# A two-block transformer kernel: one class of 21 places for weights and working tiles, in place of many classes and hand-written sequences

## The chip, the cores and the metric

The kernel runs on one core of a Trainium2 chip. The metric is the device time of one execution in microseconds (us). The profile of one execution shows the engines TensorE (PE, with its weight loads PEld), VectorE (DVE), ScalarE (ACT), GpSimd (POOL) and SyncE (SP), and the DMA queues.

## The reference

256 tokens of 1024 features, in fp32, pass two blocks. The first block has two layers, the second block one:

```python
def first_block(x, ...):
    h = x
    for l in range(DEPTH):          # DEPTH = 2
        h = h + hybrid_mixer(rmsnorm(h, norm_mix[l]), w_in[l], w_branch_a[l], w_branch_b[l],
                             b_gate[l], sink_logit[l], w_out[l])
        h = h + expert_choice_ffn(rmsnorm(h, norm_ffn[l]), w_router[l], w_expert_gate[l],
                                  w_expert_up[l], w_expert_down[l])
    return rmsnorm(h, norm_final)

def second_block(x, c, ctx, ...):
    x = x + sincos_2d(x.shape[1])
    ...
    x_mix, _, _ = token_mixer(modulate(rms_norm(x, norm1_g), sh1, sc1) @ w_in, ...)
    x = x + gt1 * x_mix
    x = x + gt2 * hier_moe(modulate(rms_norm(x, norm2_g), sh2, sc2), ...)
    return rms_norm(x, final_norm_g)
```

`hybrid_mixer` is a dilated attention and a windowed attention with a gate for each, projected by w_out. In `expert_choice_ffn` each of 16 experts takes its best 32 tokens (gate and up, 1024 x 2048, silu, down 1024 x 1024). `token_mixer` is a gated linear attention beside a long convolution; `hier_moe` has 32 experts of width 512 in 4 groups, of which each token uses 2 of one group. The weights are read once, some 750 MB in all.

## The kernel before

All weights come as chunks of 128 x 2048 fp32 (1 MB), by `Core.chunk`, whose DMA is issued by SP (`piece`, L60). A chunk can also come as four pieces of 128 x 512 in small tiles (`quarters`, L68). All other DMAs of the kernel are on SP too. The products of the mixers are made in three passes of split numbers (`mm3`, L118 to L120): ACT writes the high part `wh` (L98), DVE or POOL the low part `wl` (L99); the small classes wh and wl have three tiles of 128 x 512 each, P and PT four. The experts multiply without a split (L774, L816; in the second block L1429, L1470).

SBUF holds 19 places of 8 KB per partition for chunks and big working tiles. They are classes by tag: w (5), x (4) and ten single ones, hTa, hTb, qa, qb, qc, V, G, hgw, hn and ob. A working tile (queries, values, gates, the normed tokens) names its tag. A chunk takes its tag from `K.spare`, a list written for the stage, and when that is empty from `K.ring`, a sequence that goes round. Both are written out by hand for each stage:

```python
    own = ("hn", "ob") if ahead else ("G", "V")
    K.ring = list("wwxwx")
    K.spare = [None] * 7 + ["V", "qa", "qb", "qc"] + ([] if ahead else ["ob"]) + ["hgw"] + (["G"] if ahead else [])
    K.spare += [("P",) * 4] + ([] if ahead else ["hn"]) + [("wh", "wh", "wh", "wl"), ("wl", "wl", "PT", "PT")]
```

A tile framework finds the waits between the instructions and fixes the order of the instructions on each engine beforehand, from a plan of times of its own. A tile of a class gets a place when the place's last tenant is done with, and the tiles of one class get their places in the order in which the program writes them first. Classes are independent of each other in this.

The stages in order: `mixer` of layer 0 and `experts` of layer 0, with part of the next layer's mixer done within (`Ahead`); the same for layer 1, with preparations of the second block within (`prep`); `token_mixer`; `moe` with `moe_round` and `moe_quad`; `final`. At the end of a mixer comes w_o in two halves of 512 columns (c = 0, 1); `route` transposes the finished half of h (L190), copies it to `hTr` and multiplies it by the router (L659) between the two. Then `experts` has the scaled tokens `ht2` written (`scaled_tokens`, L677), makes the one-hot matrices, gathers each expert's tokens in `xT`, and runs over 16 experts of 8 chunks (w_eg) and 4 x 16 chunks of w_ed. `moe` writes its scaled tokens as `ht0` and `ht1` (L109) and then runs over 8 quads of 16 chunks w2eg and 8 of w2ed. Between routing and experts stand the chunks of the modulation (`ada`, and `gb` at L599).

Of the kernel before, what the change touches and what calls it, by code (L numbers as in the profile page):

```python
# [32 lines left out]
class Core:  # L33
    def __init__(self, ctx, tc, A):
        self.tc, self.nc, self.A = tc, tc.nc, A
        self.const = ctx.enter_context(tc.tile_pool(name="const", bufs=1))
        self.sb = ctx.enter_context(tc.tile_pool(name="sb", bufs=1))
        self.ps = ctx.enter_context(tc.tile_pool(name="ps", bufs=1, space=PSUM))
        self.flip = self.nsplit = self.nchunk = 0
        self.after = nullcontext  # L40
        self.ring, self.spare, self.idle = list("wwxwx"), [], ()
# [33 lines left out]
    def t(self, shape, name, bufs=1, tag=None, dt=F):  # L75
        return self.sb.tile(shape, dt, name=name, tag=tag or name, bufs=bufs)
# [134 lines left out]
class Ahead:  # L211
# [78 lines left out]
RING = {"w": 5, "x": 4}  # L290
# [25 lines left out]
def mixer(K, h, l, ada, first=None, ahead=None):  # L316
# [142 lines left out]
    if ahead:  # L459
        K.ring = list("wwwwwx")  # L460

    def window():
# [155 lines left out]
def first_loads(K):  # L618
# [3 lines left out]
    K.sink, K.bgate = K.load("sink", [128, L, 16, 2]), K.load("bgate", [128, L, 16])  # L622
# [3 lines left out]
    K.iota, K.fold = K.load("iota", [128, 65]), K.load("fold", [128, 96])  # L626
# [54 lines left out]
def experts(K, h, l, mix, ada, prep, ahead=None):  # L681
# [74 lines left out]
    K.ring = list("wwxwx")  # L756
    K.spare = [None] * 7 + ["V", "qa", "qb", "qc"] + ([] if ahead else ["ob"]) + ["hgw"] + (["G"] if ahead else [])
    K.spare += [("P",) * 4] + ([] if ahead else ["hn"]) + [("wh", "wh", "wh", "wl"), ("wl", "wl", "PT", "PT")]
    hid, Ge = [], []
    gw = K.t([128, 4], "gw4")  # L760
    for e in range(NE):
        if e == 2:
            for _ in gather(1):
                pass
            K.ring = ["w", "x", "w", "V", "w", "x", "qb", "w", "qc", "x", "w", "hgw", "x", "G"] if ahead else list("wwxwx") + ["qc"]
        oh, xT = ohs[e // 8], xTs[e // 8]
        gu = K.bank("mm")
        for k in range(KD):
# [3 lines left out]
            w = K.chunk(A["w_eg"][l, e, k])  # L772
# [34 lines left out]
    K.ring = ["w", "x", "w", "qc", "w", "x", "w", "x", "w"] if ahead else ["w", "x", "w", "qc", "w", "hTa", "x", "w", "qa", "w"]  # L807
# [25 lines left out]
    K.ring = list("wwxwx")  # L833
# [22 lines left out]
def context(K):  # L856
# [24 lines left out]
    s0 = K.t([128, PW], "S0", tag="x", bufs=RING["x"])  # L881
# [47 lines left out]
def long_filter(K):  # L929
# [29 lines left out]
    dec, hs = K.t([128, 4, 512], "dec", tag="hgw"), K.t([128, 4, 512], "hs", tag="x", bufs=RING["x"])  # L959
# [24 lines left out]
def token_mixer(K, h):  # L984
# [22 lines left out]
    cb = K.t([128, 4, 256], "cb", tag="cA")  # L1007
# [49 lines left out]
    xa = K.t([128, 8, T], "xa", tag="x", bufs=RING["x"])  # L1057
    xb = K.t([128, 8, T], "xb", tag="x", bufs=RING["x"])
# [12 lines left out]
    def hyena():  # L1071
# [29 lines left out]
        y = K.t([128, 2, 4, T], "yb", tag="x", bufs=RING["x"], dt=FR)  # L1101
# [176 lines left out]
def moe(K, h, mix):  # L1278
# [22 lines left out]
    lg = K.t([128, 2, 36], "lg2")  # L1301
# [3 lines left out]
    s = K.t([128, 2, 64], "rsm")  # L1305
# [16 lines left out]
    tmp = K.t([128, 2, NE2], "rtmp")  # L1322
# [4 lines left out]
    ix = K.t([128, 2, 8], "ix")  # L1327
# [86 lines left out]
def moe_quad(K, h, xT, oh, cmb, e, i, gate):  # L1414
# [45 lines left out]
    for hf in range(2):  # L1460
# [3 lines left out]
        wd = [K.chunk(A["w2ed"][e + x, hf]) for x in range(3 if end else 4)]  # L1464
# [94 lines left out]
def constants():  # L1559
# [15 lines left out]
    o["iota"] = np.broadcast_to(np.arange(65, dtype=f), (128, 65))  # L1575
# [30 lines left out]
def pack_first(i):  # L1606
# [28 lines left out]
    o["sink"] = np.broadcast_to(i["sink_logit"][None, :, :, None], (128, L, 16, 2))  # L1635
# [60 lines left out]
```

## Time and profile before

| | us |
|---|---|
| median of 3 runs (lowest, highest) | 2268.3 (2260.67, 2269.16) |
| the profiled execution | 2264.96 |
| its span | 2263.2 |
| PE busy | 1810.0 (80%) |
| PEld busy | 1026.7 (45%) |
| DVE busy | 786.9 (35%) |
| ACT busy | 588.7 (26%) |
| POOL busy | 220.7 (10%) |

The DMA queue of SP moved 745.82 MB; its packets took 81.7% of the 16 DMA engines' span. A DMA share near 1 in a stretch says that the 16 engines were busy throughout. A row of a timeline is one instruction, or several of a form in sequence (x7): start, time from the first to the end of the last, line, operation, output and input. A row of SP is the issue of a DMA, not its transfer. In brackets stands the idle time before an instruction and what ended it.

### The profile page before, as it was taken

The numbers are of one execution on the slowest core, as the hardware profiler recorded it, in microseconds if no ns is written. First come the engines' busy times: TensorE is split into PE (matmuls) and PEld (weight loads), VectorE is DVE, ScalarE is ACT, GpSimd is POOL, SyncE is SP. The second block draws the span as 40 slices with busy tenths as digits, with TensorE's granted clock in tenths as the row PEclk, the third lists the DMA queues.
The fourth block names the chain that finished last, engine by engine and source line by source line (L and its number), as shares of the span: only waits on it lengthen the run. The fifth ranks groups of instructions, "written<-read, shape, count | busy, mean of one in ns | idle before, by whom it ended". The sixth has DMA issues, their size and how long they took to land.

```text
span 2263.2 us, 30298 instructions
## 1 busy us (share of the span) xinstructions
PE 1810.0 (80%) x12172; PEld 1026.7 (45%) x12172; DVE 786.9 (35%) x1823; ACT 588.7 (26%) x1182; POOL 220.7 (10%) x179
## 2 busy tenths in 40 slices
PE   8999997666699998996778566669999877776765
PEld 8877741111277765842234223248888522121211
DVE  5766620000145589631211111147647511111112
ACT  5545510000033345620124200036325310000000
POOL 2111200000011122200000000024224100000000
PEclk9999997777799999998899777889999999999999
DMA  7446599999999944679999999982336799999996
GB/s 301 136 165 238 216 377 421 421 421 422 422 375 409 386 163 187 233 278 366 411 416 415 371 420 421 420 336 105 119 115 233 300 411 421 421 421 421 422 421 277
DMA packets 113626, 748.87 MB, mean 331 GB/s; under 512 B 14695, under 2 KB 15112, under 8 KB 25416
## 3 DMA queue, kind: packets, MB, share of 16 engines
q1 hardware_dynamic: 112936, 745.82, 81.7%
q8 instruction: 98, 1.61, 0.3%
q10 hardware_dynamic: 544, 1.05, 0.1%
q14 instruction: 48, 0.39, 0.1%
HBM read 745.77 MB, written 1.05 MB: 330 GB/s over the span
## 4 chain that ended last, share of the span: by engine, by line
PE 44%; DMA 27%; issue 21%; DVE 5%; ACT 2%; POOL 0%; POOLq 0%; SPq 0%; DVEq 0%; ACTq 0%
DMA w<-in_w_eg 15%; DMA w<-in_w_ed 7%; PE mm L118 7%; PE mm L120 7%; PE mm L119 6%; PE mm L774 4%; PE acc L816 4%; DMA w<-in_w2z 1%; DVE wl L99 1%; PE acc L493 1%; PE acc L901 1%; PE sc L841 1%; DMA w<-in_ada 1%; PE acc L1181 1%; PE sc L478 1%
## 5 line engine op out<-in xcount | busy, mean ns | idle before, releaser
L774 PE MATMUL mm<-w,xT 128*32 128x512 f32 x2048 | 325.0, 743 | 131.4 <-DMA w<-in_w_eg 131.3
L98 ACT ACTIVATE wh<-w 128x512 fp32r<-128x512 f32 x384 | 239.5, 630 | 314.5 <-PE mm L119 237.1
L118 PE MATMUL mm<-hTa,wh 128*128 128x256 f32 x960 | 282.5, 296 | 8.3 <-DVE qa L242 2.4
L120 PE MATMUL mm<-hTa,wl 128*128 128x256 f32 x960 | 276.4, 291 | 4.5 <-DVE wl L99 4.2
L119 PE MATMUL mm<-hTb,wh 128*128 128x256 f32 x960 | 274.4, 287 | 1.2 <-DVE hTb L1004 1.2
L99 DVE TENSOR_TENSOR wl<-w,wh 128x512 fp32r<-128x512 f32 x286 | 220.1, 775 | 100.4 <-ACT wh L98 97.5
L1429 PE MATMUL mm<-w,xT 128*32 128x512 f32 x1024 | 174.1, 618 | 61.5 <-DMA w<-in_w2eg 60.9
L99 POOL TENSOR_TENSOR wl<-w,wh 128x512 fp32r<-128x512 f32 x98 | 129.7, 1324 | 917.2 <-ACT wh L98 411.8
L774 PEld LDWEIGHTS mm<-w,xT 128*32 128x32 f32 x2048 | 59.1, 123 | 352.3 <-DMA w<-in_w_eg 245.3
L816 PE MATMUL acc<-w,hid 128*32 128x256 f32 x2048 | 167.0, 436 | 59.9 <-DMA w<-in_w_ed 59.9
L118 PEld LDWEIGHTS mm<-hTa,wh 128*128 128x128 f32 x960 | 182.8, 191 | 28.4 <-issue 13.5
L120 PEld LDWEIGHTS mm<-hTa,wl 128*128 128x128 f32 x960 | 182.5, 191 | 14.3 <-issue 6.2
L119 PEld LDWEIGHTS mm<-hTb,wh 128*128 128x128 f32 x960 | 183.5, 191 | 5.4 <-issue 2.4
L816 PEld LDWEIGHTS acc<-w,hid 128*32 128x32 f32 x2048 | 76.8, 124 | 136.2 <-DMA w<-in_w_ed 68.2
L1470 PE MATMUL acc<-w,work 128*32 128x512 f32 x512 | 103.4, 681 | 36.4 <-DMA w<-in_w2ed 35.0
L1429 PEld LDWEIGHTS mm<-w,xT 128*32 128x32 f32 x1024 | 33.6, 110 | 172.1 <-DMA w<-in_w2eg 126.1
L175 POOL TENSOR_TENSOR rs<-rs,mhalf 128x2 f32<-128x2 f32 x9 | 6.7, 748 | 1010.7 <-DVE rs L174 1010.5
L790 DVE TENSOR_TENSOR hid<-tp,sg 128x256 f32<-128x256 f32 x32 | 13.6, 424 | 221.0 <-ACT sg L789 221.0
L88 DVE COPY gs<-mm 128x512 f32<-128x512 f32 x16 | 11.1, 692 | 199.6 <-PE mm L774 199.6
L110 DVE SCALAR_TENSOR_TENSOR yd<-acc,gw,yd 128x256 fp32r<-128x256 f32 x32 | 15.5, 483 | 179.4 <-ACT yd L109 179.4
L789 ACT ACTIVATE sg<-tp 128x256 f32<-128x256 f32 x32 | 12.3, 383 | 227.5 <-PE tp L786 227.4
L109 ACT ACTIVATE yd<-acc,gw 128x256 fp32r<-128x256 f32 x32 | 15.1, 473 | 213.2 <-PE acc L816 213.2
(469 smaller groups left out, 2504.4 us busy)
## 6 DMA issues: line engine op xcount, KB each, us to landing
w<-in_w_eg SPq DMA_DIRECT2D x250, 1024.0 KB, 15.6
w<-in_w_ed SPq DMA_DIRECT2D x128, 1024.0 KB, 14.1
w<-in_w2eg SPq DMA_DIRECT2D x126, 1024.0 KB, 19.8
w<-in_w2ed SPq DMA_DIRECT2D x63, 1024.0 KB, 19.8
w<-in_ada SPq DMA_DIRECT2D x24, 1024.0 KB, 6.3
w<-in_w_in SPq DMA_DIRECT2D x22, 1024.0 KB, 7.1
w<-in_wk SPq DMA_DIRECT2D x20, 1024.0 KB, 9.3
w<-in_w_b SPq DMA_DIRECT2D x8, 1024.0 KB, 6.2
```

The costliest lines, as they stand in the source:

```text
L98: self.hi = nc.scalar.activation(hi, src, AF.Copy)
L99: (nc.gpsimd if n in self.idle or n % 4 == 3 else nc.vector).tensor_tensor(lo, src, hi.bitcast(F), OP.subtract)
L118: mm(out, lhsT=l[0], rhs=r[0], start=start, stop=False)
L119: mm(out, lhsT=l[0], rhs=r[1], start=False, stop=False)
L120: mm(out, lhsT=l[1], rhs=r[0], start=False, stop=stop)
L478: nc.tensor.matmul(p[:, sl], lhsT=q[hq], rhs=KL[hq, kv // 2, :], start=False, stop=True)
L493: nc.tensor.matmul(po[half * 64:half * 64 + 64, :T], lhsT=V[:, kt, c:c + 64], rhs=PTs[half][:, kt * 256:(kt + 1) * 256], start=(kt == 0), ...
L774: nc.tensor.matmul(gu[32 * j:32 * j + 32, :], lhsT=xT[:, k, (e % 8) * CAP:(e % 8 + 1) * CAP], rhs=w[:, j * 512:(j + 1) * 512], start=(k == ...
L816: nc.tensor.matmul(dn[32 * x:32 * x + 32, :T], lhsT=hid[e // 8][:, e % 8, f, hh * 32:hh * 32 + 32], rhs=ws[x][:, fb * T:(fb + 1) * T], sta ...
L841: nc.tensor.matmul(p[:, :T], lhsT=hn[:, tt, kb * 128:(kb + 1) * 128], rhs=oh[:, tt].rearrange("p a b -> p (a b)"), start=(tt == 0), stop=( ...
L1429: nc.tensor.matmul(gu[o:o + 32, :], lhsT=xT[:, k, y:y + CAP2], rhs=ws[x][:, (2 * kk + j) * 512:(2 * kk + j + 1) * 512], start=(k == 0), st ...
L1470: nc.tensor.matmul(dn[32 * x:32 * x + 32, :], lhsT=hid[x][:, c, :], rhs=wd[x][:, c * 512:(c + 1) * 512], start=(c == 0), stop=(c == 3), ti ...
```

## The change

All big working tiles and all whole chunks have one tag, "W", with 21 places; the hand-written sequences are gone. `experts` requests the first 21 chunks (19 whole, the ninth and tenth as quarter pieces) before the tiles that it gathers into, and `moe` does so with 16 chunks of w2eg and 3 of w2ed. The two further places come from a smaller reserve for dynamic DMAs (`dynamic_dma_scratch_size`, to 1024), a sink constant without its doubled column, a shorter iota, and small tiles of `moe` that lie in a free part of `cb`.

```diff
-        self.ring, self.spare, self.idle = list("wwxwx"), [], ()
+        self.idle, self.spare = (), []
...
-        tag = self.spare.pop(0) if self.spare else None
-        if tag is None:
-            tag = self.ring[self.nchunk % len(self.ring)]
-            self.nchunk += 1
-        if isinstance(tag, tuple):
-            return self.quarters(src, tag)
-        return self.piece(src, tag)
-
-    def piece(self, src, tag):
-        t = self.sb.tile([128, PW], F, name="w", tag=tag, bufs=RING.get(tag, 1))
+        if self.spare and (tags := self.spare.pop(0)):
+            return self.quarters(src, tags)
+        t = self.sb.tile([128, PW], F, name="w", tag="W", bufs=PLACES)
         self.nc.sync.dma_start(out=t[:, :src.shape[1]], in_=src)
         return t
+
+    def next_chunk(self, src):
+        return self.pre.pop(0) if self.pre else self.chunk(src)
...
     def t(self, shape, name, bufs=1, tag=None, dt=F):
-        return self.sb.tile(shape, dt, name=name, tag=tag or name, bufs=bufs)
+        tag = tag or name
+        if tag in WHOLE:
+            tag, bufs = "W", PLACES
+        return self.sb.tile(shape, dt, name=name, tag=tag, bufs=bufs)
...
-RING = {"w": 5, "x": 4}
+
+WHOLE = {"x", "hTa", "hTb", "qa", "qb", "qc", "V", "G", "hgw", "hn", "ob"}
+PLACES = 21
+SPARE = [None] * 8 + [("P", "P", "wh", "wh"), ("wh", "wl", "wl", "wl")]
...
-                sk = K.sink[:, l, hd, :]
+                sk = K.sink[:, l, hd:hd + 1].to_broadcast([128, 2])
...
     own = ("hn", "ob") if ahead else ("G", "V")
-    K.ring = list("wwxwx")
-    K.spare = [None] * 7 + ["V", "qa", "qb", "qc"] + ([] if ahead else ["ob"]) + ["hgw"] + (["G"] if ahead else [])
-    K.spare += [("P",) * 4] + ([] if ahead else ["hn"]) + [("wh", "wh", "wh", "wl"), ("wl", "wl", "PT", "PT")]
+    K.spare = SPARE[:]
+
+    ws = [K.chunk(A["w_eg"][l, i // KD, i % KD]) for i in range(PLACES)]
...
-            w = K.chunk(A["w_eg"][l, e, k])
+            w = ws.pop(0) if ws else K.chunk(A["w_eg"][l, e, k])
...
-    cb = K.t([128, 4, 256], "cb", tag="cA")
+    cb = K.t([128, 5, 256], "cb", tag="cA")
+    K.small = cb[:, 4]
...
-    K.spare = ["x"] * 3
     ada_gate(K, 0)
-    K.ring, K.spare = ["w"], [None] * 4 + ["x"] * 3
...
-    K.spare = ["qa", "V", "qb", "G", "hgw", "x", "x", "ob", "x", "w", ("wh", "wh", "wh", "wl"),
-               ("wl", "wl", "PT", "PT"), "qc", "w", "w", "w", "w"]
-    K.ring = ["qa", "w", "qb", "hgw", "w", "x", "ob", "w", "x", "qc", "w", "x", "w"]
+    K.spare = SPARE[:]
+    K.pre = [K.chunk(A["w2eg"][0 + 2 * i + x, c]) for i in range(2) for c in range(4) for x in range(2)]
+    K.pre += [K.chunk(A["w2ed"][x, 0]) for x in range(3)]
...
-            ws = [K.chunk(A["w2eg"][e + 2 * pr + x, c]) for x in range(2)]
+            ws = [K.next_chunk(A["w2eg"][e + 2 * pr + x, c]) for x in range(2)]
...
-    nc = bacc.Bacc("TRN2", target_bir_lowering=False, num_devices=1)
+    nc = bacc.Bacc("TRN2", target_bir_lowering=False, num_devices=1, dynamic_dma_scratch_size=1024)
```

Five more assignments of `K.ring` in the stages are removed in the same way, and tiles that named `RING["x"]` drop it.

## Rows read from the trace of the kernel before

**Rows 1.** The page: the span.

```profile
span 2263.2 us, 30298 instructions
```

**Rows 2.** Stretches: window, us; busy PE, PEld, DVE, ACT, POOL; PEclk, DMA share, GB/s.

```profile
230.00:300.00 70.00, 65.36 (x376) 45.15 (x374) 38.48 (x87) 27.96 (x54) 15.52 (x14) 0.93 0.59 224
300.00:640.00 340.00, 234.91 (x1518) 68.72 (x1516) 29.29 (x59) 25.35 (x51) 2.58 (x2) 0.78 1.01 419
640.00:800.00 160.00, 153.95 (x1432) 118.17 (x1430) 84.00 (x130) 50.98 (x89) 21.04 (x16) 0.98 0.95 384
...
1250.00:1270.00 20.00, 12.21 (x68) 5.42 (x68) 5.69 (x19) 9.58 (x12) 0.00 (x0) 0.66 0.71 279
```

**Rows 3.** The chain of waits: start us, length us, what was waited for.

```profile
366.83 19.82 DMA w<-in_w_eg
```

**Rows 4.** DMA issues, 60 to 300 us: the queue's total; count, size, us to landing.

```profile
q1 hardware_dynamic: 7950, 46.91, 53.4%
...
w<-in_w_eg SPq DMA_DIRECT2D x19, 1024.0 KB, 6.1
...
w<-in_w_eg SPq DMA_DIRECT2D x6, 256.0 KB, 6.8
```

**Rows 5.** DMA issues, 810 to 1034 us.

```profile
q1 hardware_dynamic: 9192, 47.12, 56.8%
...
w<-in_w_eg SPq DMA_DIRECT2D x26, 1024.0 KB, 6.6
...
w<-in_w_eg SPq DMA_DIRECT2D x12, 256.0 KB, 8.9
```

**Rows 6.** DMA issues, 1510 to 1820 us.

```profile
q1 hardware_dynamic: 9163, 55.19, 47.3%
...
w<-in_w2eg SPq DMA_DIRECT2D x19, 1024.0 KB, 6.7
```

**Rows 7.** SP's timeline, 230 to 300 us: start, us, what is issued.

```profile
230.73 35.59 SPq L60 DMA_DIRECT2D w<-in_w_eg  x7
266.90 3.37 SPq L68 DMA_DIRECT2D w<-in_w_eg  x6
```

**Rows 8.** ACT's timeline, 270 to 285 and 1774 to 1786 us: first writes of ht.

```profile
275.36 2.54 ACT L677 ACTIVATE ht<-h,rs 128x512 f32<-128x512 f32 x4
...
1781.62 2.56 ACT L109 ACTIVATE ht<-h,rs 128x512 fp32r<-128x512 f32 x4 [0.49 <-POOL rs L175]
```

**Rows 9.** SP's waits, 230 to 300 us: us in total, times, longest.

```profile
SPq L68 <- PE mm L120: 1.8, 3, 0.7
```

**Rows 10.** PE's timeline, 250 to 270 us: w_o (sc, mm) and route's transposes (tp).

```profile
254.13 0.64 PE L118 MATMUL sc<-wh,mTa 128*128 128x512 f32 x2
...
258.33 0.38 PE L190 MATMUL tp<-ident,h 128*128 128x128 f32 x2
...
260.59 0.64 PE L118 MATMUL mm<-wh,mTa 128*128 128x512 f32 x2
...
261.99 0.63 PE L118 MATMUL mm<-wh,mTa 128*128 128x512 f32 x2
...
269.27 0.40 PE L120 MATMUL mm<-wh,mTb 128*128 128x512 f32 x1
```

**Rows 11.** SP's timeline, 930 to 1034 us.

```profile
973.46 2.89 SPq L68 DMA_DIRECT2D w<-in_w_eg  x5
979.17 20.86 SPq L60 DMA_DIRECT2D w<-in_w_eg  x6
```

**Rows 12.** PE's and SP's timelines, 1740 to 1822 us.

```profile
1775.86 0.64 PE L118 MATMUL mm<-wh,mTa 128*128 128x512 f32 x2
...
1778.17 1.40 SPq L68 DMA_DIRECT2D w<-in_w2eg  x3
1786.66 2.04 SPq L60 DMA_DIRECT2D w<-in_w2eg  x3
```

**Rows 13.** DVE's timeline, 1465 to 1530 us: the wait is in brackets.

```profile
1496.16 2.36 DVE L994 TENSOR_TENSOR hg<-h,gf 128x1024 f32<-128x1024 f32 x2 [8.03 <-DMA gf<-in_gfin]
```

More of the change, by code (lines that the diff above doesn't have):

```diff
@@ L223, in start @@
         self.Ga, self.Gb = K.t([128, 8, T], "Ga", tag="G"), K.t([128, 8, T], "Gb", tag="hgw")
-        self.raw = K.t([128, 8, T], "raw", RING["x"], tag="x")
+        self.raw = K.t([128, 8, T], "raw", tag="x")
     def dest(self, j):
@@ L458, in mixer @@
     ob = (K.t([128, 8, T], "ob0", tag="hn", dt=FR), K.t([128, 8, T], "ob1", tag="ob", dt=FR))
-    if ahead:
-        K.ring = list("wwwwwx")
     def window():
@@ L517, in gates @@
             yield
-    QS = [K.t([128, 8, T], "q0", tag="qc", dt=FR), K.t([128, 8, T], "q1", RING["x"], tag="x", dt=FR)]
-    kx = K.t([128, 8, T], "kx", RING["x"], tag="x", dt=FR)
+    QS = [K.t([128, 8, T], "q0", tag="qc", dt=FR), K.t([128, 8, T], "q1", tag="x", dt=FR)]
+    kx = K.t([128, 8, T], "kx", tag="x", dt=FR)
     KK, KL = kx[:, 0:4, :].rearrange("p (x j) t -> p x j t", x=2), kx[:, 4:6, :]
@@ L606, in spread_gate @@
     if g == 0:
-        K.gt = K.t([128, PW], "gt", tag="x", bufs=RING["x"]).rearrange("p (a b) -> p a b", a=2)
+        K.gt = K.t([128, PW], "gt", tag="x").rearrange("p (a b) -> p a b", a=2)
     for c in range(2):
@@ L621, in first_loads @@
     nc.sync.dma_start(out=K.negd, in_=A["negd"])
-    K.sink, K.bgate = K.load("sink", [128, L, 16, 2]), K.load("bgate", [128, L, 16])
+    K.sink, K.bgate = K.load("sink", [128, L, 16]), K.load("bgate", [128, L, 16])
     K.gffn = K.load("gffn", [128, L, KD])
@@ L625, in first_loads @@
     nc.sync.dma_start(out=K.wr, in_=A["wr"])
-    K.iota, K.fold = K.load("iota", [128, 65]), K.load("fold", [128, 96])
+    K.iota, K.fold = K.load("iota", [128, CAP2 + 1]), K.load("fold", [128, 96])
     ada_setup(K)
@@ L764, in experts @@
                 pass
-            K.ring = ["w", "x", "w", "V", "w", "x", "qb", "w", "qc", "x", "w", "hgw", "x", "G"] if ahead else list("wwxwx") + ["qc"]
         oh, xT = ohs[e // 8], xTs[e // 8]
@@ L806, in experts @@
             K.copy(Ge[-1].rearrange("p a b -> p (a b)"), p)
-    K.ring = ["w", "x", "w", "qc", "w", "x", "w", "x", "w"] if ahead else ["w", "x", "w", "qc", "w", "hTa", "x", "w", "qa", "w"]
     for q in range(4):
@@ L832, in experts @@
                 next(prep, None)
-    K.ring = list("wwxwx")
 def gather_x(K, xT, hn, oh, gain, bias=None):
@@ L880, in context @@
     yield
-    s0 = K.t([128, PW], "S0", tag="x", bufs=RING["x"])
+    s0 = K.t([128, PW], "S0", tag="x")
     K.S0 = s0[:, :1024].rearrange("p (d h v) -> p d h v", d=2, h=HG)
@@ L958, in long_filter @@
     nc.sync.dma_start(out=w3, in_=A["hw3"])
-    dec, hs = K.t([128, 4, 512], "dec", tag="hgw"), K.t([128, 4, 512], "hs", tag="x", bufs=RING["x"])
+    dec, hs = K.t([128, 4, 512], "dec", tag="hgw"), K.t([128, 4, 512], "hs", tag="x")
     nc.sync.dma_start(out=dec, in_=A["decay"])
@@ L1056, in token_mixer @@
     weave((project_qv(), 16), (scans(), 8))
-    xa = K.t([128, 8, T], "xa", tag="x", bufs=RING["x"])
-    xb = K.t([128, 8, T], "xb", tag="x", bufs=RING["x"])
+    xa = K.t([128, 8, T], "xa", tag="x")
+    xb = K.t([128, 8, T], "xb", tag="x")
     hy = [xa[:, 0:4, :], xa[:, 4:8, :], xb[:, 0:4, :]]
@@ L1100, in hyena @@
                 yield
-        y = K.t([128, 2, 4, T], "yb", tag="x", bufs=RING["x"], dt=FR)
+        y = K.t([128, 2, 4, T], "yb", tag="x", dt=FR)
         for c in range(4):
@@ L1300, in moe @@
     cmb, msk, slot = R[:, 0], R[:, 1], R[:, 2]
-    lg = K.t([128, 2, 36], "lg2")
+    lg = K.small[:, 0:72].rearrange("p (t e) -> p t e", t=2)
     for tt in range(2):
@@ L1304, in moe @@
                                        op0=OP.mult, op1=OP.add)
-    s = K.t([128, 2, 64], "rsm")
+    s = K.small[:, 72:168].rearrange("p (t e) -> p t e", t=2)
     m, sm, pg, den = s[:, :, 0], s[:, :, 1], s[:, :, 2], s[:, :, 3]
@@ L1321, in moe @@
     le = lg[:, :, NG:36].rearrange("p t (g e) -> p t g e", g=NG)
-    tmp = K.t([128, 2, NE2], "rtmp")
+    tmp = K.small[:, 168:232].rearrange("p (t e) -> p t e", t=2)
     nc.vector.tensor_tensor(tmp.rearrange("p t (g e) -> p t g e", g=NG), le,
@@ L1325, in moe @@
     nc.vector.tensor_reduce(el, tmp.rearrange("p t (g e) -> p t e g", g=NG), axis=AX.X, op=OP.add)
-    ix = K.t([128, 2, 8], "ix")
+    ix = K.small[:, 232:248].rearrange("p (t e) -> p t e", t=2)
     ixu = K.t([128, 2, 8], "ixu", dt=mybir.dt.uint32)
@@ L1463, in moe_quad @@
         end = e + 4 + hf == NE2 + 1
-        wd = [K.chunk(A["w2ed"][e + x, hf]) for x in range(3 if end else 4)]
+        wd = [K.next_chunk(A["w2ed"][e + x, hf]) for x in range(3 if end else 4)]
         if end:
@@ L1574, in constants @@
     o["ident"] = np.eye(128, dtype=f)
-    o["iota"] = np.broadcast_to(np.arange(65, dtype=f), (128, 65))
+    o["iota"] = np.broadcast_to(np.arange(CAP2 + 1, dtype=f), (128, CAP2 + 1))
     s = np.arange(128)
@@ L1634, in pack_first @@
     o["bgate"] = i["b_gate"].reshape(L, 16, 128).transpose(2, 0, 1)
-    o["sink"] = np.broadcast_to(i["sink_logit"][None, :, :, None], (128, L, 16, 2))
+    o["sink"] = np.broadcast_to(i["sink_logit"][None], (128, L, 16))
     wr = i["w_router"].reshape(L, KD, 128, NE).transpose(2, 0, 1, 3)
```

## The prediction

> **What bounds the kernel now.** I read the span first, then the table of stretches, then the chain of waits, then the DMA issues and SP's timeline ahead of each expert stage.
>
> The profiled execution took 2264.96 us, with a span of 2263.2 us [rows 1]. The median of the three runs is 2268.3 us, 3.3 us more; the sum is made against the profiled execution and its result is taken for the median, within that 3.3 us. About 0.5%, 11.3 us, is what a measurement of this kernel can tell from no change.
>
> The stretches [rows 2] show two kinds of stage. In the expert stages (300 to 640 us, and three more stretches like it) the DMA share is 1.01 at 419 GB/s, and TensorE is busy for 234.91 us of 340: the weights bound them. The chain of waits [rows 3] says the same: steps of 19.82 us, one after another, that wait for w_eg. Eight chunks of 1 MB (1.0486 million bytes) pass in one such step, so **a chunk costs 2.48 us**. Between the stages it is the other way round: from 230 to 300 us TensorE is busy for 65.36 us of 70 and the DMA share is 0.59 [rows 2]. What a stage costs is thus set by how many of its chunks have already come in when it turns DMA-bound. Each chunk less by then is 2.48 us more at the end, and the reverse. So the change is priced by counting chunks at three edges: 300, 1034 and 1820 us.
>
> **Chunks at the edges, before.** By the DMA issues from 60 to 300 us [rows 4], 46.91 MB went through the queue, 44.7 chunks; 25 are other weights (nine of w_in, seven of ada, four each of w_b and w_o, one of w_a) and about 0.7 had been issued earlier, which leaves **19** of w_eg (20.5 issued: 19 whole and six quarters). From 810 to 1034 us [rows 5] 47.12 MB are 44.9 chunks, less 15 of the mixer and 1.4 of small loads: **28.5** (26 whole, twelve quarters and a 1 MB constant issued). From 1510 to 1820 us [rows 6] 55.19 MB are 52.6 chunks, less 28 of the mixer, 1 of small loads and 1 issued earlier: **22.6** (27 whole issued, 19 of them w2eg, and twelve quarters).
>
> Where they come from is seen on SP, the one queue that issues all of them [rows 7]: seven whole chunks of w_eg from 230.73 us on, within 35.59 us, then six quarter pieces from 266.90 us. That is well before the stage has its own tiles: ht2, the scaled tokens, is first written at 275.36 us, in the last stage at 1781.62 us [rows 8]. The old kernel can do that since each kind of place is a class with an order of its own: a w_eg for V's or qa's place passes a tile that waits for another class.
>
> **Part 1: one class in program order.** The framework gives the places of one class out in the order in which its tiles are first written in the program, and fixes the order on each engine beforehand by a plan. In that plan a request behind a tile that has no writer yet stands still, even if a place is free. With every big tile in "W", w_eg's requests stand behind ht2 (in the last stage behind the two parts of ht). The quarter pieces of the ninth and tenth chunk belong to P, wh and wl, other classes. They pass, and are planned when wh and wl come free, which is when the last products of w_o have read them; in the trace SP's pieces wait for those products three times, 1.8 us in all [rows 9]. So the order on SP becomes: w_o, ada, **pieces**, and only then w_eg 0 and what follows. On the chip SP stops at the first piece until w_o's last split is used, though places are free, and everything behind it on SP stops too. The rest of the change cannot help there.
>
> The end of w_o moves as well. In the old order the products of its second half (mm) begin when those of the first (sc) end, at 254.8 us, are mixed with the transposes of route (L190, 258.33 us) and end at 269.7 us [rows 10]. Its two chunks are requested after hTr, which is now in the same class, and hTr's first write follows those transposes. So in the plan the second half comes whole behind the transposes and L659. From 254.8 us add 8 groups of 1.40 us (the distance of the rows at 260.59 and 261.99 us [rows 10]), 11.2 us, and about 8 us for the sum into h, the transposes, copies and L659 (the transposes begin 3.5 us after the first half, and copies and L659 are taken to need as much again and 1 us): 274 us, some **4.5 us later**.
>
> Layer 0: the six pieces that went from 266.90 us within 3.37 us [rows 7] go 4.5 us later, to 274.8 us, and w_eg 0 follows. To 300 us the queue carries 25.2 / 2.48 = 10.1 chunks, with the two of pieces 12.1, against 19. 6.9 chunks x 2.48 = **+17 us**.
>
> Layer 1: the pieces that wait for w_o go at 973.46 us and six whole chunks from 979.17 us, with others ahead of them [rows 11]. After, the pieces end near 981 us (4.5 us later, and 2.9 us to issue) and w_eg 0 follows. To 1034 us that is 53 / 2.48 = 21.4 and two of pieces, less 0.5 for the small loads: 22.9 against 28.5, 5.6 x 2.48 = +13.9 us. Given back: from 1250 to 1270 us the DMA share is 0.71 [rows 2], 5.8 us idle, in a join between w_eg and w_ed where a tag had no place; with one class that should go: -5.8. **+8 us**.
>
> Last stage: the last products of w2o begin at 1775.86 us; the last pieces went at 1778.17 and whole chunks again at 1786.66 us [rows 12]. Route's part is longer here (64 columns for 32), so I take 6 us for the 4.5: the pieces at 1782 to 1785, w2eg 0 at 1786. To 1820 us 34 / 2.48 = 13.7, and two: 15.7 against 22.6, 6.9 x 2.48 = **+17 us**.
>
> **Part 2: two places more, 21 for 19, and the small reserve freed.** While the share is 1.01 a deeper queue carries nothing more: 0. From 640 to 800 us, where w_ed and the next layer's first weights share the places, the share is 0.95 [rows 2]: 8 us idle, of which two places and free choice can win from 0 to all; I take half, **-4 us**. The shrunken reserve serves dynamic DMAs, of which this kernel has none on its path; no row shows it waiting; from -2 to +2 us, 0 taken.
>
> **Part 3: joins.** At the passage to the second block DVE waits 8.03 us for gf [rows 13], which stood on SP behind a chunk without a place. Program order puts it earlier; but ada's chunks then stand behind gb. From -8 to +2, taken **-2**. At the start the small constants may wait behind the first chunks: 0 to +4, taken **+2**. The broadcast of sink, the shorter iota and small tiles in cb change one operand each of DVE and ACT under a TensorE that is busy 65.36 us of 70 [rows 2]: 0; if that cover were gone, 32 heads by a tenth of a us.
>
> **Sum:** 17 + 8 + 17 - 4 - 2 + 2 = +38; 2265 + 38 = 2303, and with a third of the 3.3 us to the median **2304 us**.
>
> **A rule against the trace.** The stretches show the expert stages with a full DMA [rows 2], so that TensorE's gaps there are paid by bandwidth. The Trainium skill's page "Perfetto Trace Analysis", section Identifying Performance Opportunities, says that a gap which repeats on the engine that should be saturated can mean that memory for the next tile is missing; by that rule more places would fill the gaps and the change would win, which is the first rival.
>
> **Rivals.** *Faster: the prefetch is not held.* If the pieces are planned behind w_eg 0 to 7, the places that a mixer frees are filled at once: 21 chunks in layer 0 and 19 whole ones with two quartered elsewhere, 2 to 4 more than now by each edge. That is -5 to -10 us for each of three stages, with -5.8 and -4 from the idle stretches [rows 2]: about -25, **2243 us**. For it: the idle DMA from 230 to 300 us is there to be used. Against it: w_eg still comes after ht2 in the program, and the pieces belong to classes that pass. It decides if w_eg 0 to 7 are issued before 265 us in layer 0.
> *No change.* The pieces hold SP only half as long, as w_o's end doesn't move: 8 + 3 + 8, less 4, 6 and 3: about +6, **2272 us**. It would need both halves of part 1 to be overstated.
> *Slower still.* The mixers' own weights, too, stand behind tiles of the class (raw, kx, q1), and TensorE, at 65.36 of 70 us there, waits: 10 us in each of two to three mixers, +60 in all, **2325 us**. Against it: share 0.59 leaves room.
>
> **How the numbers follow.** The forecast, 0.52; slower still, 0.12; no change, 0.12; faster, 0.24. The forecast's own range is 2280 to 2322 (each of the three edges by 2 chunks, the joins by their ends). With the rivals on either side 2244 to 2328 leaves 2 in 10 out. Faster 0.24, same 0.13, slower 0.63.
>
> **What would show it.** Right: on SP, whole w_eg issues in one burst only behind quarter pieces near 271, 980 and 1786 us; DMA nearly idle from 250 to 270 us; 12, 23 and 16 chunks at the three edges; L190 on TensorE ahead of the second half of w_o; the 8.03 us at L994 shorter; the join near 1250 us full. Wrong: whole w_eg issues between 230 and 265 us, ahead of ht2's first write; or expert stages that begin with 19 chunks or more and end earlier than now.

## The result, and the profile after

The changed kernel takes 2355.5 us (median of 4 runs, 2354.7 to 2363.1) against 2268.7 us: ratio 1.040, 95% interval 1.036 to 1.043. It is **slower by 87 us**; 36 were forecast, and the range ended at 2328. The profiled execution has a span of 2354.4 us, 91.2 more than that of before [rows 1].

The stretches of the changed kernel, with the columns of [rows 2]:

```profile
230.00:300.00 70.00, 60.74 (x368) 48.37 (x368) 39.30 (x77) 33.39 (x65) 18.53 (x17) 0.95 0.44 168
300.00:640.00 340.00, 228.66 (x1351) 58.79 (x1354) 24.02 (x65) 17.40 (x36) 0.00 (x0) 0.79 1.01 420
667.00:827.00 160.00, 155.02 (x1479) 122.27 (x1478) 86.63 (x135) 54.26 (x94) 22.38 (x17) 1.00 0.99 405
1250.00:1380.00 130.00, 102.64 (x598) 39.30 (x594) 18.30 (x49) 43.35 (x57) 0.00 (x0) 0.84 1.01 419
```

The expert stages are as DMA-bound as before (1.01, 420 GB/s). The two stretches with idle time in the kernel before, 640 to 800 and 1250 to 1270 us, lie 27 and some 45 us later now; there the share is 0.99 and 1.01, so most of that idle time is gone, as forecast. What is lost lies ahead of the stages: from 230 to 300 us the queue moved 168 GB/s where it had moved 224. SP's timeline of the changed kernel says why, in all three places (start, time to the last issue, line, DMA):

```profile
205.36 14.42 SPq L64 DMA_DIRECT2D w<-in_w_o  x8
219.88 1.33 SPq L53 DMA_DIRECT2D w<-in_w_b  x3
258.16 1.48 SPq L64 DMA_DIRECT2D w<-in_w_eg  x2
259.69 0.90 SPq L53 DMA_DIRECT2D w<-in_w_o  x2
260.64 1.81 SPq L53 DMA_DIRECT2D w<-in_ada  x3
282.56 3.58 SPq L64 DMA_DIRECT2D w<-in_w_eg  x6
286.18 133.12 SPq L53 DMA_DIRECT2D w<-in_w_eg  x59
...
994.05 1.47 SPq L64 DMA_DIRECT2D w<-in_w_eg  x2
...
1018.33 3.59 SPq L64 DMA_DIRECT2D w<-in_w_eg  x6
1021.98 66.31 SPq L53 DMA_DIRECT2D w<-in_w_eg  x32
...
1789.11 2.92 SPq L53 DMA_DIRECT2D w<-in_ada  x4
1843.12 3.12 SPq L64 DMA_DIRECT2D w<-in_w2eg  x5
...
1848.34 22.12 SPq L53 DMA_DIRECT2D w<-in_w2eg  x14
```

The order is the forecast one: pieces (L64), then all whole chunks of w_eg, one after another. But the first w_eg goes out at 286.18 us, not 274.8; before, seven had gone from 230.73 us on [rows 7]. The pieces hold SP not once but twice: from 221 to 258 us (the first two, and behind them w_o's own second half and ada), and again until 282.56 us. The first two are of class P, whose places the pieces of w_o's first half (class P, too) hold until they are split; the other six are of wh and wl. SP's waits, 255 to 290 us and 1840 to 1930 us (us in total, times, longest), where [rows 9] has 1.8 us in all:

```profile
SPq L64 <- DVE wl L98: 54.4, 2, 36.9
...
SPq L64 <- DVE wl L98: 48.4, 1, 48.4
```

The DMA issues of the changed kernel from 60 to 300 us, for [rows 4]: 30.49 MB are 29.1 chunks; less seven of w_in, seven of ada, four each of w_b and w_o and one of w_a, 6 of w_eg are in, where 12 were forecast and 19 had been. At the last edge, 1820 us, nothing of w2eg has been issued yet.

```profile
q1 hardware_dynamic: 5907, 30.49, 35.5%
...
w<-in_w_eg SPq DMA_DIRECT2D x11, 1024.0 KB, 16.7
...
w<-in_w_eg SPq DMA_DIRECT2D x8, 256.0 KB, 4.4
```

TensorE's order at the end of w_o, for [rows 10] (L189 is route's transposes, L659 the router, L117 a product of w_o):

```profile
270.67 0.44 PE L189 MATMUL tp<-ident,h 128*128 128x128 f32 x2 [0.32 <-DVE h L547]
271.27 0.88 PE L189 MATMUL tp<-ident,h 128*128 128x128 f32 x6 [0.16 <-DVE h L547]
272.40 1.52 PE L659 MATMUL acc<-hTr,wr 128*32 128x256 f32 x8 [0.25 <-DVE hTr L89]
273.85 0.73 PE L117 MATMUL mm<-wh,mTa 128*128 128x512 f32 x2
...
285.10 0.40 PE L119 MATMUL mm<-wh,mTb 128*128 128x512 f32 x1
```

The second half of w_o now stands whole behind transposes and router, as forecast, and takes 11.6 us. The scaled tokens follow at 291.19 us in place of 275.36 [rows 8].

To tell stages apart, the span is cut at the first write of ht2, at the last product of w_ed (L814), at the first product with fold behind the second block's router, and at the last product of w2ed. Each cut is a start in the view of one line's instructions (count, shortest/median/longest ns, first to last start), like these of the changed kernel:

```profile
L677 ACT ACTIVATE ht<-h,rs x4: 704/706/706, 291.2 to 293.0; 128x512 f32<-128x512 f32 x4
...
L814 PE MATMUL acc<-w,hid x870: 379/379/634, 639.6 to 825.3; 128*32 128x256 f32 x174
...
L677 ACT ACTIVATE ht<-h,rs x4: 705/706/706, 1026.9 to 1028.8; 128x512 f32<-128x512 f32 x4
...
L814 PE MATMUL acc<-w,hid x1024: 379/403/636, 1374.4 to 1535.7; 128*32 128x256 f32 x171
...
L1466 PE MATMUL acc<-w,work x512: 589/592/1062, 1894.8 to 2337.2; 128*32 128x512 f32 x171
```

The same cuts for every profiled execution give this table, in us (the kernels of the experiments are told below):

| stage | before | after | e1 | e2 | e3 | e4 | e5 | e6 | e9 | e10 |
|---|---|---|---|---|---|---|---|---|---|---|
| mixer of layer 0 | 275.4 | 291.2 | 288.2 | 285.4 | 286.0 | 287.1 | 284.2 | 274.8 | 271.5 | 272.8 |
| experts of layer 0 | 523.2 | 534.1 | 516.8 | 534.3 | 515.4 | 513.4 | 515.3 | 512.8 | 534.0 | 512.4 |
| mixer of layer 1 | 182.6 | 201.6 | 196.5 | 188.9 | 192.0 | 190.2 | 191.4 | 193.8 | 196.7 | 187.9 |
| experts of layer 1 | 501.3 | 508.8 | 487.6 | 506.9 | 488.9 | 487.7 | 489.3 | 485.4 | 510.0 | 487.3 |
| token mixer | 302.4 | 316.3 | 316.6 | 310.4 | 309.6 | 313.9 | 312.5 | 299.6 | 301.1 | 301.4 |
| last expert stage | 461.8 | 485.2 | 482.6 | 484.6 | 482.8 | 459.8 | 470.2 | 464.6 | 484.0 | 460.7 |

So the changed kernel loses 15.8 + 19.0 + 13.9 = 48.7 us in the mixers and 10.9 + 7.5 + 23.4 = 41.8 us in the expert stages; 0.7 us is left for the end. The loss has two halves, and the experiments were made to part them.

### The profile page after: what moved, and what is told of

Read it like the earlier page. It is cut to its first block, busy times and chain, and to the rows that moved or that the text cites. A ratio compares the mean times of both kernels' runs of the same rounds, so it can differ in the third digit from the quotient of the medians.

```text
span 2354.4 us, 30290 instructions
## 1 busy us (share of the span) xinstructions
PE 1865.7 (79%) x12172; PEld 1043.7 (44%) x12172; DVE 779.2 (33%) x1823; ACT 585.4 (25%) x1181; POOL 217.6 (9%) x179
## 5 line engine op out<-in xcount | busy, mean ns | idle before, releaser
L773 PE MATMUL mm<-w,xT 128*32 128x512 f32 x2048 | 336.4, 755 | 130.2 <-DMA w<-in_w_eg 129.2
L117 PE MATMUL mm<-hTa,wh 128*128 128x256 f32 x960 | 284.1, 297 | 14.6 <-ACT wh L97 9.3
L98 DVE TENSOR_TENSOR wl<-w,wh 128x512 fp32r<-128x512 f32 x286 | 210.7, 750 | 105.7 <-ACT wh L97 102.9
L1425 PE MATMUL mm<-w,xT 128*32 128x512 f32 x1024 | 179.2, 621 | 73.9 <-DMA w<-in_w2eg 73.1
L814 PE MATMUL acc<-w,hid 128*32 128x256 f32 x2048 | 177.4, 448 | 62.6 <-DMA w<-in_w_ed 62.5
L773 PEld LDWEIGHTS mm<-w,xT 128*32 128x32 f32 x2048 | 50.8, 121 | 346.3 <-DMA w<-in_w_eg 292.8
L117 PEld LDWEIGHTS mm<-hTa,wh 128*128 128x128 f32 x960 | 185.4, 193 | 36.2 <-issue 14.9
L814 PEld LDWEIGHTS acc<-w,hid 128*32 128x32 f32 x2048 | 81.2, 128 | 145.2 <-DMA w<-in_w_ed 81.9
L1425 PEld LDWEIGHTS mm<-w,xT 128*32 128x32 f32 x1024 | 34.9, 111 | 197.0 <-DMA w<-in_w2eg 145.1
L789 DVE TENSOR_TENSOR hid<-tp,sg 128x256 f32<-128x256 f32 x32 | 13.6, 425 | 229.9 <-ACT sg L788 229.9
L788 ACT ACTIVATE sg<-tp 128x256 f32<-128x256 f32 x32 | 12.3, 384 | 230.7 <-PE tp L785 230.7
```

The costliest lines, as they stand in the source:

```text
L98: (nc.gpsimd if n in self.idle or n % 4 == 3 else nc.vector).tensor_tensor(lo, src, hi.bitcast(F), OP.subtract)
L117: mm(out, lhsT=l[0], rhs=r[0], start=start, stop=False)
L773: nc.tensor.matmul(gu[32 * j:32 * j + 32, :], lhsT=xT[:, k, (e % 8) * CAP:(e % 8 + 1) * CAP], rhs=w[:, j * 512:(j + 1) * 512], start=(k == ...
L789: nc.vector.tensor_mul(hid[-1][:, e % 8], pv[:, :, 64:128], sg)
L814: nc.tensor.matmul(dn[32 * x:32 * x + 32, :T], lhsT=hid[e // 8][:, e % 8, f, hh * 32:hh * 32 + 32], rhs=ws[x][:, fb * T:(fb + 1) * T], sta ...
L1425: nc.tensor.matmul(gu[o:o + 32, :], lhsT=xT[:, k, y:y + CAP2], rhs=ws[x][:, (2 * kk + j) * 512:(2 * kk + j + 1) * 512], start=(k == 0), st ...
```

## The experiments

The kernel before was measured anew beside each group of runs: 2268.7 us beside the changed kernel, 2263.5 beside e1 to e4, 2265.4 beside e5 to e8 and 2267.5 beside e9 to e11. A difference between groups is thus known to some 5 us. A stage time of the table comes from a single execution: e8, whose weights and places are those of the kernel before, has 464.9 us for the last stage where that has 461.8.

**e1, no pieces.** The quarter pieces ahead are left out; 19 whole chunks are asked for at once.

```diff
-SPARE = [None] * 8 + [("P", "P", "wh", "wh"), ("wh", "wl", "wl", "wl")]
+SPARE = []
...
-    ws = [K.chunk(A["w_eg"][l, i // KD, i % KD]) for i in range(PLACES)]
+    ws = [K.chunk(A["w_eg"][l, i // KD, i % KD]) for i in range(PLACES - 2)]
...
-    K.pre += [K.chunk(A["w2ed"][x, 0]) for x in range(3)]
+    K.pre += [K.chunk(A["w2ed"][x, 0]) for x in range(1)]
```

> The changed kernel with no quarter pieces of w_eg and w2eg ahead (19 whole chunks asked for at once). Theory A (SP stands at the pieces until the products of w_o have read wh and wl, and the whole prefetch behind them stands too): w_eg 0 goes out right behind ada, near 263 us instead of 286 in layer 0 and some 23 us earlier in layer 1; w2eg 0 near 1793 less the shift, instead of 1848. By the chunks that this carries earlier: about -18, -18 and -40 us, 2280 us in all. Rival B (the prefetch would stand anyway behind the first write of ht2, or is late only because the mixers are late): w_eg 0 still goes out at 286 us, 2355 us.

2310.8 us, 45 less than the changed kernel. The hold is real: the two first expert stages are 17.3 and 21.2 us shorter (table). The prefetch starts 63 us earlier, before w_o's end and not behind it, since the first two pieces no longer stand ahead of w_o and ada; it then waits for places. Places were free in that time: from 221 to 258 us, while SP of the changed kernel stands at the first piece, e1 issues ten chunks of w_eg. The stretch in the changed kernel, then in e1:

```profile
221.00:258.00 37.00, 33.00 (x255) 31.90 (x255) 21.28 (x39) 22.77 (x45) 12.47 (x12) 0.95 0.25 95
221.00:258.00 37.00, 33.00 (x247) 31.55 (x246) 22.63 (x41) 21.38 (x44) 13.96 (x13) 0.95 1.01 420
```

SP's timeline of e1, layer 0 and the last stage:

```profile
219.84 1.61 SPq L53 DMA_DIRECT2D w<-in_ada  x3
223.06 197.17 SPq L53 DMA_DIRECT2D w<-in_w_eg  x69
...
1741.00 2.91 SPq L53 DMA_DIRECT2D w<-in_ada  x4
1795.64 3.35 SPq L64 DMA_DIRECT2D w<-in_w2ed  x4
...
1799.52 25.87 SPq L53 DMA_DIRECT2D w<-in_w2eg  x16
```

The last stage did not gain (482.6 us), and its rows show why: four pieces of w2ed (L64), the very last chunk of the kernel, stand on SP ahead of w2eg 0, with 52 us between ada and them. They are of wh and wl, asked for at the end of the program, and passed everything as pieces do.

**e2, weights before tiles.** Pieces kept; the mixers' chunks of w_b (w2b) are asked for before mT, those of w_o's second half (and w2o) before hTr.

```diff
+    wb = [K.chunk(A["w_b"][l, c]) for c in range(4)]
     mT = K.pair("mT")
...
+    wo = [[K.quarters(A["w_o"][l, i], [tag] * 4) for i, tag in enumerate(("P", "PT"))],
+          [K.chunk(A["w_o"][l, 2]), K.chunk(A["w_o"][l, 3])]]
     for c in range(2):
...
-        K.row_blocks(ws, mT, add, ("sc", "mm")[c])
+        K.row_blocks(wo[c], mT, add, ("sc", "mm")[c])
...
```

> The changed kernel, pieces kept, with the chunks of w_b (w2b) asked for before mT and those of w_o's second half (w2o) before hTr. Theory: TensorE's order at w_o becomes the mixed one of before again, worth 4 to 5 us in each of the two layers and 8 in the second block, and the waits at the second chunk of w_b (2.3 us each) go: -20 to -25 us, 2332 us. Rival (the order on TensorE is free, since the pieces hold SP as before): within 5 us of 2355.

2325.9 us, 29.5 less, a little more than expected. The gain lies in the mixers (5.8, 12.7 and 5.9 us); the expert stages stay within 2 us of the changed kernel's. TensorE's products of w_o are mixed with route's again. e1 and e2 thus take away different halves, in the main.

**e3, both edits.**

> Both edits: no pieces, and w_b and w_o asked for before mT and hTr. If the two costs are apart, they add: 2355 - 75 - 22 = 2258 us, about the kernel before. If the earlier w_o only shortens the same hold, the two overlap and it stays at 2275 or above.

2292.4 us, 63 less, where 45 + 29.5 = 74 would be the sum: most of it adds, 11 us overlap (6 when every time is set against the kernel before of its own group). It misses the 2258 expected by the last stage, still held by the pieces of w2ed (482.8 us).

**e5, e3 with the last chunk of w2ed whole.**

```diff
-        wd = [K.next_chunk(A["w2ed"][e + x, hf]) for x in range(3 if end else 4)]
-        if end:
-            wd.append(K.quarters(A["w2ed"][e + 3, hf], ("wh", "wh", "wh", "wl")))
+        wd = [K.next_chunk(A["w2ed"][e + x, hf]) for x in range(4)]
```

> e3 with the last chunk of w2ed whole too. In e1 and e3 the four quarter pieces of that last chunk, which are used only at the very end, stand on SP ahead of w2eg 0 (at 1781 us in e3), as they belong to wh and wl. Theory A: they hold the last stage just as the pieces of w_eg did, and with them gone w2eg 0 goes out behind ada near 1737 us instead of 1787; the stage then begins with 15 to 17 chunks instead of 5: -25 to -35 us against e3, 2262 us; a whole last chunk costs 1 to 2 us at the end. Rival: w2eg waits for free places anyway, within 5 us of 2292.

2279.4 us, 13 less than e3, half of what was expected. w2eg 0 goes out at 1773.77 us instead of 1786.91, not at 1737: the next small class stands in the way. SP's waits in e5 from 1733 to 1775 us, and then the issues in its timeline:

```profile
SPq L598 <- ACT mTa L105: 23.1, 1, 23.1
SPq L598 <- POOL h L1269: 15.3, 1, 15.3
```

```profile
1733.10 1.86 SPq L53 DMA_DIRECT2D w<-in_ada  x4
1773.39 0.33 SPq L598 DMA_DIRECT2D gb<-in_gtb  x1
1773.77 22.73 SPq L53 DMA_DIRECT2D w<-in_w2eg  x16
```

L598 is gb, whose place is one of P. By the releasers that the view names it waits 38 us for instructions that write mTa and h, and w2eg waits behind it.

**e4, early.** e3 with the first 12 chunks (EARLY) of the next stage asked for in the mixer, right behind w_o (and w2eg likewise behind w2o).

```diff
           [K.chunk(A["w_o"][l, 2]), K.chunk(A["w_o"][l, 3])]]
+    K.pre = [K.chunk(A["w_eg"][l, i // KD, i % KD]) for i in range(EARLY)]
...
-    ws = [K.chunk(A["w_eg"][l, i // KD, i % KD]) for i in range(PLACES - 2)]
+    ws, K.pre = K.pre + [K.chunk(A["w_eg"][l, i // KD, i % KD]) for i in range(EARLY, PLACES - 2)], []
```

> As e3, with the first 12 chunks of the next expert stage asked for in the mixer, right behind w_o. Theory A: SP then has chunks to issue while w_o is multiplied, before the ada chunks; where free places allow, each stage begins with 2 to 4 chunks more: -5 to -10 us per stage against e3, about 2240 us, below the kernel before. Rival C (the places are not free before w_o's end, so that asking earlier moves nothing): within 5 us of e3.

2263.1 us, ratio 0.9999 (0.9987 to 1.0012) to the kernel before, where 2240 was expected. The expert stages are now **shorter** than before, by 9.8, 13.6 and 2.0 us; the last one lost its hold (459.8 us), since w2eg now stands ahead of ada, gb and the pieces. What is left are the mixers, 11.7, 7.6 and 11.5 us longer than before. The two first stages hardly differ from e3, as rival C has it: there places were the limit.

**e7, e4 with 19 places** (and two chunks less asked for).

```diff
-PLACES = 21
-EARLY = 12
+PLACES = 19
+EARLY = 10
...
-    K.pre += [K.chunk(A["w2eg"][i // 8 * 2 + i % 2, i % 8 // 2]) for i in range(EARLY, 16)]
-    K.pre += [K.chunk(A["w2ed"][x, 0]) for x in range(1)]
+    K.pre += [K.chunk(A["w2eg"][i // 8 * 2 + i % 2, i % 8 // 2]) for i in range(EARLY, 15)]
```

> e4 with 19 places instead of 21 (two chunks less ahead in each stage). If what counts is the number of chunks that are in when a stage turns DMA-bound, two less in each of three stages cost 2 x 2.48 x 3 = 15 us: 2278 us. If a free place is never what is missing, within 4 us of 2263.

2283.1 us, 20 more than e4 (18 against the kernels before of the two groups), where 15 had been expected. The profiled executions are only 9 us apart, as that of e4 was one of its slowest and that of e7 its fastest: in them the three expert stages are 3.9, 4.9 and 4.5 us longer, 13.3 in all, and the mixers 4 us shorter. So in the expert stages the two further places are worth about what two chunks a stage cost, once the prefetch is not held; the rest of the 20 us is not parted. What they are worth while it is held was not run: the changed kernel with 19 places is missing.

**e6, early and looked ahead.** e4 with the last chunk of w2ed whole, w_in asked for four chunks ahead of use and the second block's projections two.

```diff
-        w_in = iter(A["w_in"])
+        w_in = Lookahead(K, [A["w_in"][i] for i in range(1, A["w_in"].shape[0])], 4)
         x = K.pair("hT")
...
-            K.col_blocks(K.chunk(next(w_in)), KD, x, emit_qw, 2 * c)
+            K.col_blocks(next(w_in), KD, x, emit_qw, 2 * c)
...
+class Lookahead:
...
+    def fill(self):
+        while self.srcs and len(self.q) < self.n:
+            self.q.append(self.K.chunk(self.srcs.pop(0)))
...
+    def __next__(self):
+        self.fill()
+        w = self.q.pop(0)
+        self.fill()
+        return w
```

> e4 with the last chunk of w2ed whole, and in the mixers each chunk of w_in asked for four chunks ahead (before hT, qa, V, q1 and kx), those of the second block's projections two ahead. Theory: the 3 us wait of TensorE near 18 us, the waits for the split of a chunk just landed (5.5 and 5.6 us in the second block) and the late clock go, and the last stage's second part of the prefetch is not held: -4 for the start, -5 in the first mixer, -5 in the second block, -5 in the last stage, 2244 us, below the kernel before by about 1%. Rival D (the mixers are longer because the plan orders TensorE differently, not for late chunks): within 6 us of e4's 2263.

2246.4 us, ratio 0.991 (0.989 to 0.994): below the kernel before. The mixers of layer 0 and the second block give 12.3 and 14.3 us back and are as short as before; that of layer 1 (193.8 us) and the last stage (464.6) do not gain. The start shows the first of it: in the changed kernel, as in e4, the constants pass the first whole chunks of w_in, as those stand behind hT and qa, and TensorE waits 2.6 us for a split near 20 us. SP's row of these chunks, before and after:

```profile
5.74 3.02 SPq L60 DMA_DIRECT2D w<-in_w_in  x5
15.95 21.91 SPq L53 DMA_DIRECT2D w<-in_w_in  x15
```

Two stretches of the kernel before, of the changed kernel, of e10 and of e1, one after the other:

```profile
0.00:50.00 50.00, 42.88 (x318) 41.71 (x319) 26.45 (x57) 25.67 (x45) 11.56 (x13) 0.97 0.83 319
125.00:175.00 50.00, 50.00 (x340) 40.09 (x338) 33.38 (x119) 24.16 (x68) 6.43 (x5) 1.00 0.40 143
```

```profile
0.00:50.00 50.00, 39.96 (x288) 38.22 (x289) 24.55 (x53) 23.75 (x42) 11.33 (x13) 0.97 0.88 336
125.00:175.00 50.00, 49.68 (x297) 35.03 (x296) 33.23 (x126) 23.58 (x75) 3.84 (x3) 0.93 0.30 106
```

```profile
0.00:50.00 50.00, 42.82 (x317) 41.45 (x318) 24.79 (x57) 25.32 (x45) 11.17 (x13) 0.97 0.87 337
125.00:175.00 50.00, 50.00 (x338) 37.76 (x338) 34.42 (x122) 24.34 (x74) 5.14 (x4) 1.00 0.41 141
```

```profile
0.00:50.00 50.00, 40.09 (x290) 38.46 (x291) 24.68 (x53) 23.88 (x42) 11.48 (x13) 0.97 0.88 338
125.00:175.00 50.00, 49.68 (x314) 35.45 (x315) 33.50 (x126) 24.54 (x75) 5.12 (x4) 1.00 0.31 106
```

TensorE is busy for 2.9 us less in the first 50 us of the changed kernel, and its granted clock from 125 to 175 us is 0.93 instead of 1.00 of the upper level (2.4 GHz); in e10, with the chunks asked for ahead, both are as before. But the one does not bring the other along by itself: e1 has the same late start and a granted clock of 1.00 there. In the same 49.68 us of busy time its rows count 314 products, those of the changed kernel 297, and its mixer of layer 0 is 3.0 us shorter.

**e9, the mixers alone.** The changed kernel with its pieces, and e2's edit and the look-ahead of e6; the next layer's wk are asked for at the start of its mixer.

```diff
         x = ahead.x
+        ahead.want(3)
         ahead.turned(3)
...
+    def want(self, q):
+        for c in (0, 1, 5, 2, 3, 4):
+            self.got[q, c] = self.take(q, c)
...
-        w = K.chunk(K.A["wk"][q, c] if c < 4 else K.A["wk6"][q])
+        w = self.take(q, c)
```

> The changed kernel with its quarter pieces kept as they are, and only the mixers' own weights asked for early: w_b before mT, w_o before hTr, w_in four chunks and the second block's projections two chunks ahead, the next layer's wk at the start of its mixer. Theory: the three mixers, 15.8, 19.0 and 13.9 us longer than before, come back to within 3 us each, and the expert stages keep their 10.9, 7.5 and 23.4 us, as the prefetch is still held: 2355 - 46 = 2309 us. Rival (the longer mixers come from the held queue, not from late requests): as e2, 2326 us or more.

2313.9 us, 41.5 less. The expert stages keep what they had (534.0, 510.0, 484.0 us), and the mixers of layer 0 and the token mixer are at or below before. The mixer of layer 1 keeps 14 us too much; in e10, without the hold, 5. That the hold is the reason isn't shown: in e2, with the hold and without the look-ahead, it kept only 6. This part is open.

**e10 and e11, all of it.** e4 with the look-ahead, the last chunk of w2ed in pieces again (the edit against e6); e10 with the early wk, e11 without.

```diff
-        wd = [K.next_chunk(A["w2ed"][e + x, hf]) for x in range(4)]
+        wd = [K.next_chunk(A["w2ed"][e + x, hf]) for x in range(3 if end else 4)]
+        if end:
+            wd.append(K.quarters(A["w2ed"][e + 3, hf], ("wh", "wh", "wh", "wl")))
```

> e4 (no pieces of w_eg and w2eg, 12 chunks asked for in the mixer) with the mixers' weights asked for early as in e9, and the last chunk of w2ed in pieces as before. In e6 that chunk was whole, and its last stage took 464.6 us from the routing against 459.8 in e4: -5 us against e6. The mixer of layer 1, which e6 left 11 us longer than before: -8 us. 2246 - 13 = 2233 us, 1.5% below the kernel before. If the pieces at the end hold more than they save, and the mixer's length has another cause: 2246 or above.

> As e10, without the early requests of wk: tells its two terms apart. 2241 us if the last chunk's pieces are worth 5 us; 2246 or above if they cost.

e10 takes 2240.2 us, ratio 0.988 (0.986 to 0.991), the fastest of all, 27 us below the kernel before; 2233 was expected. e11 takes 2243.1 us. With the pieces at the end the last stage takes 459.8, 460.7 and 459.4 us (e4, e10, e11), without them 464.6 (e6): some 4 us, little more than single executions differ by. The early wk are worth 3 us by the medians, where 8 had been expected; layer 1's mixer took 187.9 us in e10 and 193.3 in e11, in one execution each. A stretch of e10:

```profile
230.00:300.00 70.00, 63.07 (x369) 44.08 (x368) 36.35 (x84) 26.89 (x53) 13.76 (x13) 0.95 0.83 333
```

The queue moves 333 GB/s in the stretch ahead of the stage, against 224 before and 168 in the changed kernel.

**e8, the freed reserve alone, in the kernel before.** Dynamic reserve of 1024, sink by broadcast, iota of 33; places and sequences as they were.

```diff
-    K.sink, K.bgate = K.load("sink", [128, L, 16, 2]), K.load("bgate", [128, L, 16])
+    K.sink, K.bgate = K.load("sink", [128, L, 16]), K.load("bgate", [128, L, 16])
...
-    K.iota, K.fold = K.load("iota", [128, 65]), K.load("fold", [128, 96])
+    K.iota, K.fold = K.load("iota", [128, CAP2 + 1]), K.load("fold", [128, 96])
...
-    nc = bacc.Bacc("TRN2", target_bir_lowering=False, num_devices=1)
+    nc = bacc.Bacc("TRN2", target_bir_lowering=False, num_devices=1, dynamic_dma_scratch_size=1024)
```

> The kernel before with the small reserve freed alone (dynamic reserve of 1024, sink broadcast, iota of 33), places and sequences as they were. Every theory here: no change, within 5 us of the kernel before. If the smaller reserve or the broadcast cost anything, it shows here, with nothing else changed.

2266.7 us, ratio 0.9999 (0.9982 to 1.0016): no cost that these runs could tell from nothing.

## Why the prediction was wrong

**Right: the mechanism of part 1.** The order on SP (w_o, ada, pieces, then all of w_eg) and on TensorE (second half of w_o behind transposes and router) came as forecast, at all three places; e1 shows that the pieces cause the first, e2 that the order of requests causes the second. With the hold gone and the weights of w_b and w_o asked for first the kernel is no slower than before (e4), so a single class is not what costs.

**Wrong: the size of "the end of w_o moves as well".** That step priced the mixers at 4.5, 4.5 and 6 us, for the order at w_o alone. They lost 15.8, 19.0 and 13.9. The three edges together had 42 us in the sum, 15 of them for the mixers, and measured 90.5: 33.7 of the missing 48.5 us lie in the mixers.

The order at w_o itself cost less than the step had it. From the last product of w_o's first half (sc) to the last of its second half [rows 10], 13.5 us passed before and 15.1 us after: 1.6 us more, 1.5 in layer 1 and 4.7 in the last mixer. But the first half already ended 14.2 us later, where the step, starting from 254.8 us of the old trace, had put nothing. TensorE waits 8.8 us from 14 to 258 us, 6.2 of them for the split of a chunk, where the kernel before waits 0.2. The last product of the first half before and after, and the longest of these waits:

```profile
255.76 0.40 PE L120 MATMUL sc<-wh,mTb 128*128 128x512 f32 x1
269.96 0.40 PE L119 MATMUL sc<-wh,mTb 128*128 128x512 f32 x1
...
PE mm L117 <- ACT wh L97: 4.9, 2, 2.6
```

The rule that the step itself used, that a request behind an unwritten tile stands still, holds for every other chunk of a mixer, too: the last three of w_b behind mT, w_in behind hT, qa, q1 and kx, the projections of the second block behind their tiles. e2 (24 us) and the look-ahead (27 us from e4 to e6 in two mixers) show it. The rival "slower still" had named raw, kx and q1, at 10 us more in each of two to three mixers and a chance of 0.12; its evidence against, that a DMA share of 0.59 leaves room, was the wrong row, as the queue had room and SP no request to issue. Together with the forecast's own 15 us that rival has 35 to 45 us for the mixers, near the 48.7 measured, and its 2325 us was the nearest of all the times given.

**Wrong: when the hold begins and ends.** It was priced as one wait that ends with w_o. The pieces also stand ahead of w_o's second half and ada, from 221 us on, since the first two wait for the places of P that w_o's own first half holds; and as the mixer itself ends later, so does the hold: w_eg 0 at 286.2, 1022.0 and 1848.3 us, not 274.8, 981 and 1786. In the last stage the loss from the routing on was 23.4 us where 17 - 6 = 11 were in the sum: by 35 us behind the routing, at 1887 us, the queue had carried 16.51 MB, 15 chunks without gf and gb, and not the 18 that the same working gives there. Two reasons are seen: the pieces, counted as two chunks already in, are issued only 5 us ahead of w2eg 0, and gf and gb go between. The rest was not parted further.

The DMA issues from 1843 to 1887 us, the queue's total:

```profile
q1 hardware_dynamic: 3229, 16.51, 95.7%
```

**Right: the gains; wrong: the start.** Most of the idle time of the stretches 640 to 800 and 1250 to 1270 us is gone; the forecast took half of the first. DVE waits no longer for gf at L991 (what that alone is worth, no run tells), and the freed reserve shows no cost (e8). They are real, but sum up to little beside the loss. At the start the constants were to wait behind the first chunks, at +2 us. It is the other way round: the chunks wait behind the constants, from 5.74 to 15.95 us, and TensorE waits for their split.

**The faster rival** was right on what is to be had, -25 us: e10 gives -27, and 25.9 us of it lie in the expert stages (10.8, 14.0 and 1.1, though the rival had 5 to 10 for the last, too). Its condition, that the prefetch is not held, was false for this program, and is made true by asking earlier. Here the Trainium skill's sentence on missing memory (page "Perfetto Trace Analysis", section Identifying Performance Opportunities) finds its place: by e7 two places less cost 13 us in the expert stages, in a kernel whose requests come early enough to fill them. In the changed kernel places stood free while SP waited for a tile of another class (e1's ten chunks from 221 to 258 us).

## What to carry to other kernels

Where places are given out in program order, a prefetch begins where its request stands, not where a place comes free: ask for weights before the tiles of the same class that are written late, in the small stages as well as in the large one. And on one in-order queue a request of a small class that must wait holds everything behind it, so look for what stands at the head of the queue in the timeline before counting free places. Price such a change at each place where the rule applies; the first one found was not the only one here.

## What the runs showed that was not expected

The order on one queue reaches across the whole program: a piece used only near 2270 us held the last stage's first weights at 1787 us (e3), and when it was gone a load of 256 KB did the same (e5). And two kernels can differ in TensorE's clock far from any edit: of the seven profiled executions with the late first chunk (the changed kernel, e1 to e5 and e7) six had a granted clock of 0.93 to 0.97 from 125 to 175 us and e1 had 1.00, as had all six without it. What links the two, and what spared e1, the runs don't show.
